# Eight of sixteen k-tile pairs of the down projection by the seven-product scheme instead of seven, in other places

## The chip, the core and the metric

The kernel runs on one core of a Trainium2 chip. Its engines are TensorE (PE: matrix products into PSUM; PEld is its loading of the stationary operand), VectorE (DVE), ScalarE (ACT), GpSimd (POOL) and SyncE (SP), which here only issues DMA transfers. The metric is the time of one execution on the device, in microseconds, and less is better.

## The reference

One decoder layer on 256 tokens with a width of 2048, all in float32. A recurrent branch and a sliding-window attention are merged and projected, and then comes the part that matters here, an MLP with a squared ReLU:

```python
h = rmsnorm(x, norm_mlp_pre[l])
u = jnp.square(jax.nn.relu(h @ w_mlp_up[l]))
x = x + rmsnorm(u @ w_mlp_down[l], norm_mlp_post[l])
```

`w_mlp_up` is 2048 x 8192 and `w_mlp_down` is 8192 x 2048. So the down projection sums over 8192 hidden channels, that is 64 k tiles of 128.

## The kernel before

**Products in three parts.** Every float32 operand is split into a rounded part (`hi`) and the remainder (`lo`), and a product is three matrix products: hi x hi, hi x lo and lo x hi (`product`, L1108). ScalarE rounds a weight half of 128 x 1024 (`whi`, L94), and VectorE subtracts to get the remainder (`wlo`, L95).

**The weight stream** (`Stream`, L54) handles the weights of the whole kernel in the order of their use. A weight chunk is 128 x 2048, which is two halves of 512 KB. SP loads a half into one of four raw buffers (`wraw`, L76), and the next load into that buffer can be issued only when the half has been split. The splits go to six `whi` and six `wlo` buffers, and `ahead` (L138) asks for the splits six halves ahead of the one in use. The four raw buffers mean that half j+4 is loaded into the buffer of half j.

**The MLP in two halves.** The hidden layer is done in two halves of 4096 channels (f = 0 and 1). Each half has an up projection of sixteen pairs of k tiles (`up_pair`, `a_pair`), whose results are squared and laid out by `evacuate` (L1090), and then two passes of the down projection (`down`, L1119), n = 0 and 1, for 1024 output columns each. So there are four passes. A pass goes through the sixteen pairs p = 0 to 15. The last two (14 and 15) are held back and multiplied at the end, one output quarter after the other, so that a quarter can be finished while the next is still being computed. The sums of the first half are written to DRAM (`acc_away`) and read back at the start of the first pass of the second half (L1215); the residual `x1` is read back near the end (L1226).

**Plain and seven-product pairs.** One pair p meets a 2 x 2 block problem: two token tiles by two k tiles times two k tiles by two column quarters. A plain pair takes 8 block products of three matmuls each, 24. A pair in `SEVEN` takes Strassen's scheme in Winograd's form: 7 block products, 21 matmuls. For this it needs sums of the weight blocks, and of the activation blocks:

```python
v.tensor_tensor(one..., b[:, l]..., a..., ALU.add)                 # L123, 1024 columns
v.tensor_tensor(b[:, l], t[:, l], a[:, r], ALU.add)                # L125, 512, in place
v.tensor_tensor(two, b[:, l], b[:, r], ALU.add)                    # L126, 512
self.nc.scalar.copy(hi, t)                                         # L129, 1536: thi
v.tensor_tensor(lo, t, hi.bitcast(F32), ALU.subtract)              # L130, 1536: tlo
```

These (`split_sums`, L114) stand beside the usual split of the two halves, of which the second is changed by L125. The sums `t` and their parts `thi` and `tlo` each take one of twelve large buffers (`unit`, L211, 8 KB a partition), which also hold the normalised input h2T (four), the plain pairs' activations (`rooms`, L1179), and in the last two passes the sums of the first half, the gain and `x1`. The three of `t` are used last in a pair: seven products in the order P1, Q3, P2, P6, Q4, Q5, N7 (L1112), and the last three take `thi` and `tlo`. The activations of a seven-product pair have seven blocks, with both parts, in tiles named `seven` (L1196), and `evacuate` makes their sums (L1101 to L1106).

Four products (P1, P6, Q5, N7) are kept in banks of their own through the pass. After the last pair of `SEVEN` they are combined (L1152 to L1156), in the second half the sums of the first are added (`early`, L1220), and each quarter is finished by one more addition (L1208, L1243, L1246).

**Order.** Each engine takes its instructions in a fixed order, made when the program is built by a scheduler from the order of the code and the buffers' release. `pin` keeps a few in the order of the code. An instruction that waits holds back all that stand behind it on its engine.

Of the kernel before, what the change touches and what calls it, by code (L numbers as in the profile page):

```python
# [19 lines left out]
F32R = mybir.dt.float32r  # L20
# [5 lines left out]
P = 128  # L26
# [9 lines left out]

WRAW, WHALF, T2, HELD = 4, 6, 8, 4

SEVEN = (0, 2, 4, 6, 8, 10, 12)
PAIRS = 16  # L40


# [124 lines left out]
def layer(tc, x, g_pre, pos_t, pos_row, inv_freq, vecs, sinks, gains, w_kv, w_q, w_xy, w_rg, w_g, w_rp, w_ap, w_out,  # L167
# [37 lines left out]
    for f in range(2):  # L205
        chunks += [w_up[32 * f + i] for i in range(32)]
        for n in range(2):
            sums.update(len(chunks) + i for i in SEVEN)
            chunks += [w_dn[(2 * f + n) * PAIRS + i] for i in range(PAIRS)]

    def unit(name, dt=F32R):  # L211
        return big.tile([P, 4, 2, S], dt, tag="U8", name=name)

    def flat(t):
        return t.rearrange("p a b c -> p (a b c)")
# [11 lines left out]
    def pump(n=1):  # L227

        for _ in range(n):
            while waiting:  # L230
                try:
                    next(waiting[0])
                    break
                except StopIteration:
                    waiting.pop(0)
# [7 lines left out]
    def a_pair(acts, out, prio=0):  # L243


        ps = pair("ps")

        def run(j, part, ks=range(8)):
            f, half = j // 2, j % 2
            for k in ks:  # L250
                kt = half * 8 + k
                a, w = acts[kt // 4][:, kt % 4], parts[j][part][:, k * P : k * P + P]
                if part:
                    mm(ps[:, f, 1, :], w, a[:, 0, :], start=False, stop=j == 1 and k == 7)  # L254
                else:
                    mm(ps[:, f].rearrange("p a b -> p (a b)"), w, a.rearrange("p a b -> p (a b)"), start=kt == 0,  # L256
                       stop=j == 3 and k == 7)

        at = ws.at
        parts = [ws.half()]
        run(0, 0)
        parts.append(ws.half(False))
        run(1, 0)
        pump()
        parts.append(ws.half(False))
        run(2, 0, (0,))
        run(0, 1)
        ws.ahead(at + 1)  # L270
        pump()
        run(1, 1)
        ws.ahead(at + 2)
        run(2, 1)
        parts.append(ws.half(False))
        run(3, 1)
        pump()
        run(2, 0, range(1, 8))
        ws.ahead(at + 3)
        run(3, 0)  # L280
        pump()
        with tc.high_priority(prio) if prio else ExitStack():
            nc.scalar.copy(out, ps[:, :, 1, :])
            nc.vector.tensor_tensor(out, ps[:, :, 0, :], out, ALU.add)
# [381 lines left out]
    def wide(t):  # L666
        return t.rearrange("p (f t) -> p f t", f=2)
# [208 lines left out]
    def u2(name):  # L876
        return pb.tile([P, 512], F32, tag="u2", bufs=4, name=name)
# [150 lines left out]
    for tb in range(TB):  # L1028
        for i in range(2):
            q = 2 + i  # L1030
# [3 lines left out]
    def up_pair(p, out):  # L1034

        ps = up_ps[p]
        for j in range(4 * p, 4 * p + 4):
            f, half = j // 2 % 2, j % 2
            kts = range(half * 8, half * 8 + 8)
            if j < 6:  # L1040
                lo = halves[j][1]
            else:
                hi, lo = ws.half()
                for kt in kts:
                    mm(ps[:, f].rearrange("p a b -> p (a b)"), hi[:, kt % 8 * P : kt % 8 * P + P],
                       h2T[kt // 4][:, kt % 4].rearrange("p a b -> p (a b)"), start=kt == 0, stop=False)
            for kt in kts:
                mm(ps[:, f, 1, :], lo[:, kt % 8 * P : kt % 8 * P + P], h2T[kt // 4][:, kt % 4, 0, :], start=False,
                   stop=kt == KT - 1)
            pump()  # L1050
        with tc.high_priority(PRIO):
            nc.scalar.copy(out, ps[:, :, 1, :])
            nc.vector.tensor_tensor(out, ps[:, :, 0, :], out, ALU.add)
# [28 lines left out]
    def spread_r2():  # L1082
        pr = bank(psb, "pr")
        for tb in range(TB):
            mm(pr[:, tb * P : tb * P + P], ones, diag[tb], start=True, stop=True)
        nc.scalar.copy(r2, pr[:, 0:S])
# [3 lines left out]
    def evacuate(p, u, dst):  # L1090
        nc.vector.scalar_tensor_tensor(wide(u), wide(u), 0.0, r2.unsqueeze(1).to_broadcast([P, 2, S]), ALU.max,
                                       ALU.mult)
        nc.scalar.activation(u, u, AF.Square)
        if p not in SEVEN:
            nc.scalar.copy(dst[:, :, 0, :], wide(u))
            nc.vector.tensor_tensor(dst[:, :, 1, :], wide(u), dst[:, :, 0, :].bitcast(F32), ALU.subtract)
            return

        e = u2("e")
        u4, e4 = [t.rearrange("p (a b) -> p a b", a=4) for t in (u, e)]  # L1100
        nc.vector.tensor_tensor(e4[:, 0:2], u[:, 0:P].unsqueeze(1).to_broadcast([P, 2, P]), u4[:, 1:3], ALU.subtract)  # L1101
        nc.vector.tensor_tensor(e4[:, 2], e4[:, 1], u4[:, 1], ALU.subtract)
        nc.vector.tensor_tensor(e4[:, 3], e4[:, 2], u4[:, 3], ALU.add)
        for to, of in ((dst[:, :, 0:3], u4[:, 1:4]), (dst[:, :, 3:7], e4)):
            nc.scalar.copy(to[:, 0], of)
            nc.vector.tensor_tensor(to[:, 1], of, to[:, 0].bitcast(F32), ALU.subtract)  # L1106

    def product(b, a, w, begun, tail=False):  # L1108

        for i, (x, y) in enumerate(((0, 0), (0, 1), (1, 0))):  # L1110
            mm(b, a[x], w[y], start=not begun and i == 0, stop=tail and i == 2)  # L1111
# [7 lines left out]
    def down(f, n, uT, held, order, finish, early, between=lambda p: None, behind=lambda: None):  # L1119
# [21 lines left out]
        for p in range(PAIRS - held):  # L1141
            if p in SEVEN:
                parts = ws.seven()
                for name, (i, w) in LEFT.items():
                    product(banks[name], (uT[p][:, 0, i], uT[p][:, 1, i]), parts[w], name in begun,
                            p == SEVEN[-1] and name in ("P1", "P6", "Q5", "N7"))
                    begun.add(name)
                if p == SEVEN[-1]:
                    for name in ((1, 0), (0, 0), (1, 1), (0, 1)):
# [27 lines left out]
    for f in range(2):  # L1177
        uT = {}
        rooms = [unit(f"uT{f}{i}") for i in range((PAIRS - len(SEVEN) + 1) // 2)]  # L1179
        full = []  # L1180
        for p in range(PAIRS):
            u = u2("u")
            if f == 0 and p < 2:
                up_pair(p, wide(u))
            else:
                a_pair(h2T, wide(u), PRIO if p == PAIRS - 1 else 0)
            full.append((p, u))
            if f == 0 and p == R2_AT:
                pump(99)
                spread_r2()  # L1190
                ctx3.close()
                pc = ctx2.enter_context(tc.tile_pool(name="pc", bufs=1))
            if f == 1 or p >= R2_AT:
                for q, u in full:
                    if q in SEVEN:
                        uT[q] = pc.tile([P, 2, 7, P], F32R, tag="seven", bufs=len(SEVEN), name=f"seven{f}{q}")  # L1196
                    else:
                        i = sum(k not in SEVEN for k in range(q))
                        uT[q] = rooms[i // 2][:, 2 * (i % 2) : 2 * (i % 2) + 2]
                    evacuate(q, u, uT[q])  # L1200
                full.clear()
# [142 lines left out]
```

## Time and profile before

| | us |
|---|---|
| three runs | 1510.14, 1512.02, 1512.23 (median 1512.02) |
| the profiled execution, whole | 1509.99 |
| its span, first to last instruction | 1508.2 |
| TensorE busy | 1492.7 |
| VectorE busy | 1101.7 |
| ScalarE busy | 828.7 |

The clock granted to TensorE was 0.998 of the full one. In the views, a row of the timeline gives the start, the duration, the engine, the line, the operation, the tiles written and read, and in brackets the idle time before it with what ended it. A row of the chain of work that ended last gives the start, the share of time on the chain, and what it was. A row of busy time by stretch gives the stretch, its length, and for PE, PEld, VectorE, ScalarE and GpSimd the busy time and the number of instructions, then the granted clock, the share of the DMA engines and GB/s. A matmul's listed duration is longer than the distance to the next one's start, since they overlap.

### The profile page before, as it was taken

What the parts mean: (1) busy time and instruction counts of PE and PEld (TensorE: products, weight loads), DVE (VectorE), ACT (ScalarE), POOL (GpSimd) and SP (SyncE); (2) the same over time, 40 slices, a digit from 0 to 9 for tenths busy, and PEclk for the clock granted to TensorE, in tenths of its full rate; (3) what the DMA queues carried; (4) which work ended last, traced back from release to release, by engine and by line L of the source; (5) the groups of instructions that cost most, each with busy time, mean ns of one, the idle gap of its engine ahead of it and who ended that gap; (6) DMA issues with size and microseconds to landing.
All of it is one profiled execution on the core that took longest, in us unless ns stands there. A gap on an engine that the chain in (4) does not pass through costs nothing.

```text
span 1508.2 us, 20012 instructions
## 1 busy us (share of the span) xinstructions
PE 1492.7 (99%) x7600; PEld 1261.5 (84%) x7600; DVE 1101.7 (73%) x1379; ACT 828.7 (55%) x1143; POOL 1.7 (0%) x9
## 2 busy tenths in 40 slices
PE   9999999999999999999999999999999999999997
PEld 7887787889888888888888888888888888888885
DVE  6675677858669966555667866698886666788897
ACT  6554665647566766443355655565454555555453
POOL 0000000000000000000000000000000000000000
PEclk9999999999999999999999999999999999999999
DMA  6645454465646566556764755566667565576665
GB/s 254 221 157 173 148 166 136 157 201 165 213 155 221 170 209 197 192 184 195 268 221 136 270 188 188 194 194 213 217 201 237 195 195 183 193 236 202 204 221 186
DMA packets 83327, 296.19 MB, mean 196 GB/s; under 512 B 9760, under 2 KB 10016, under 8 KB 82208
## 3 DMA queue, kind: packets, MB, share of 16 engines
q1 hardware_dynamic: 79920, 287.58, 57.6%
q10 hardware_dynamic: 3312, 7.35, 1.3%
q8 instruction: 59, 0.97, 0.3%
q14 instruction: 36, 0.29, 0.1%
HBM read 288.60 MB, written 6.29 MB: 196 GB/s over the span
## 4 chain that ended last, share of the span: by engine, by line
PE 84%; DVE 8%; DMA 4%; ACT 2%; issue 1%; DVEq 0%; SPq 0%; ACTq 0%
PE ps L256 21%; PE ps L254 11%; PE dQ L1111 5%; PE pp L298 4%; PE pp L294 4%; PE pp L296 4%; PE g L294 4%; DMA wraw<-in_w_dn 4%; PE g L298 4%; PE g L296 4%; DVE wlo L95 3%; PE s L1111 3%; PE dP L1111 2%; PE q L294 2%; PE q L298 2%; PE q L296 2%
## 5 line engine op out<-in xcount | busy, mean ns | idle before, releaser
L95 DVE TENSOR_TENSOR wlo<-wraw,whi 128x1024 fp32r<-128x1024 f32 x523 | 632.7, 1221 | 306.1 <-ACT whi L94 302.9
L94 ACT CAST whi<-wraw 128x1024 fp32r<-128x1024 f32 x523 | 544.2, 1052 | 554.0 <-PE ps L256 127.3
L256 PE MATMUL ps<-h2T,whi 128*128 128x512 f32 x960 | 223.9, 390 | 0.0
L256 PEld LDWEIGHTS ps<-h2T,whi 128*128 128x128 f32 x960 | 178.3, 188 | 35.6
L256 PE MATMUL ps<-hT,whi 128*128 128x512 f32 x512 | 121.3, 392 | 0.0
L254 PEld LDWEIGHTS ps<-h2T,wlo 128*128 128x128 f32 x960 | 119.1, 192 | 2.3
L254 PE MATMUL ps<-h2T,wlo 128*128 128x256 f32 x960 | 119.9, 283 | 0.0
L256 PEld LDWEIGHTS ps<-hT,whi 128*128 128x128 f32 x512 | 94.7, 188 | 19.8 <-issue 1.1
L1111 PE MATMUL dQ<-whi,uT 128*128 128x512 f32 x288 | 106.9, 389 | 0.0
L294 PE MATMUL g<-whi,hT 128*128 128x512 f32 x256 | 101.3, 396 | 0.0
L296 PE MATMUL g<-wlo,hT 128*128 128x512 f32 x256 | 100.1, 391 | 0.1
L298 PE MATMUL g<-whi,hT 128*128 128x512 f32 x256 | 99.9, 390 | 0.0
L254 PEld LDWEIGHTS ps<-hT,wlo 128*128 128x128 f32 x512 | 63.7, 192 | 1.8 <-issue 0.7
L254 PE MATMUL ps<-hT,wlo 128*128 128x256 f32 x512 | 64.7, 284 | 0.0
L1111 PEld LDWEIGHTS dQ<-whi,uT 128*128 128x128 f32 x288 | 54.1, 188 | 11.2
L294 PEld LDWEIGHTS g<-whi,hT 128*128 128x128 f32 x256 | 48.1, 188 | 10.5 <-issue 1.0
L296 PEld LDWEIGHTS g<-wlo,hT 128*128 128x128 f32 x256 | 48.1, 188 | 10.1 <-DVE wlo L95 0.5
L298 PEld LDWEIGHTS g<-whi,hT 128*128 128x128 f32 x256 | 48.1, 188 | 10.1
L1111 PE MATMUL dQ<-wlo,uT 128*128 128x512 f32 x144 | 56.1, 389 | 0.0
L1111 PE MATMUL dCs<-whi,uT 128*128 128x512 f32 x144 | 54.1, 389 | 0.0
L1111 PE MATMUL dP<-whi,uT 128*128 128x512 f32 x144 | 54.1, 389 | 0.0
L130 DVE TENSOR_TENSOR tlo<-t,thi 128x1536 fp32r<-128x1536 f32 x28 | 49.2, 1757 | 5.1 <-ACT thi L129 5.1
(285 smaller groups left out, 2461.6 us busy)
## 6 DMA issues: line engine op xcount, KB each, us to landing
wraw<-in_w_up SPq DMA_DIRECT2D x128, 512.0 KB, 3.9
wraw<-in_w_dn SPq DMA_DIRECT2D x128, 512.0 KB, 4.5
wraw<-in_w_g SPq DMA_DIRECT2D x64, 512.0 KB, 4.7
wraw<-in_w_xy SPq DMA_DIRECT2D x64, 512.0 KB, 3.7
wraw<-in_w_q SPq DMA_DIRECT2D x32, 512.0 KB, 4.3
wraw<-in_w_ap SPq DMA_DIRECT2D x32, 512.0 KB, 4.8
wraw<-in_w_rp SPq DMA_DIRECT2D x32, 512.0 KB, 4.6
wraw<-in_w_out SPq DMA_DIRECT2D x32, 512.0 KB, 4.9
```

Source lines behind the costliest of these rows:

```text
L94: self.pin(self.nc.scalar.copy(hi, src))
L95: self.pin(self.nc.vector.tensor_tensor(lo, src, hi.bitcast(F32), ALU.subtract))
L130: v.tensor_tensor(lo, t, hi.bitcast(F32), ALU.subtract)
L254: mm(ps[:, f, 1, :], w, a[:, 0, :], start=False, stop=j == 1 and k == 7)
L256: mm(ps[:, f].rearrange("p a b -> p (a b)"), w, a.rearrange("p a b -> p (a b)"), start=kt == 0, stop=j == 3 and k == 7)
L294: mm(banks[tb][n], a[:, 0, t], hi[:, n * 512 : n * 512 + 512], start=first, stop=False)
L296: mm(banks[tb][n], a[:, 0, t], lo[:, n * 512 : n * 512 + 512], start=False, stop=False)
L298: mm(banks[tb][n], a[:, 1, t], hi[:, n * 512 : n * 512 + 512], start=False, stop=last)
L1111: mm(b, a[x], w[y], start=not begun and i == 0, stop=tail and i == 2)
```

## The change

The tuple of seven-product pairs is replaced: 0, 2, 4, 6, 8, 10, 12 become 0, 1, 3, 5, 7, 9, 11, 13. In each of the four passes eight pairs take the scheme instead of seven; pairs 0 and 1 follow each other, and the last one is 13, directly ahead of the two held pairs. The places for the plain pairs' activations, two pairs to a unit, go from five units to four by the expression at L1179. The activation tiles of the first seven such pairs stay in their own buffers, and that of pair 13 takes a large unit, of which it uses seven of eight blocks. The layout of the weights in DRAM follows the tuple.

```diff
-SEVEN = (0, 2, 4, 6, 8, 10, 12)
+SEVEN = (0, 1, 3, 5, 7, 9, 11, 13)
+IN_POOL = 7
 PAIRS = 16
...
                     if q in SEVEN:
-                        uT[q] = pc.tile([P, 2, 7, P], F32R, tag="seven", bufs=len(SEVEN), name=f"seven{f}{q}")
+                        if SEVEN.index(q) < IN_POOL:
+                            uT[q] = pc.tile([P, 2, 7, P], F32R, tag="seven", bufs=IN_POOL, name=f"seven{f}{q}")
+                        else:
+                            uT[q] = flat(unit(f"seven{f}{q}")).rearrange("p (a b c) -> p a b c", a=2, b=8)[:, :, 0:7]
```

## The prediction

> **What bounds the kernel now.** I read the page first, then the busy time by stretch. The four down passes run from 980 to 1156 us and from 1333 to 1498 us.
>
> ```profile
> PE 1492.7 (99%) x7600; PEld 1261.5 (84%) x7600; DVE 1101.7 (73%) x1379; ACT 828.7 (55%) x1143; POOL 1.7 (0%) x9
> ...
> PE 84%; DVE 8%; DMA 4%; ACT 2%; issue 1%; DVEq 0%; SPq 0%; ACTq 0%
> ```
> ```profile
> 1156.00:1333.00 177.00, 177.00 (x1022) 156.84 (x1022) 124.00 (x147) 96.01 (x119) 0.00 (x0) 1.00 0.61 197
> 1333.00:1415.60 82.60, 82.60 (x365) 68.11 (x364) 70.22 (x69) 42.31 (x45) 0.00 (x0) 1.00 0.65 218
> 1415.60:1498.00 82.40, 82.40 (x365) 68.09 (x363) 72.97 (x77) 42.52 (x48) 0.00 (x0) 1.00 0.63 209
> 1498.00:1508.20 10.20, 0.20 (x1) 0.00 (x0) 5.86 (x11) 1.29 (x5) 0.00 (x0) 0.69 0.49 171
> ```
>
> TensorE never waits in a down pass, but VectorE is busy 85% to 89% of each of the last two. The chain that ended last, read in order of time, says more: it leaves TensorE at 1318.81 and does not come back.
>
> ```profile
> 1318.81 1.63 PE ps L256 x7
> ...
> 1412.37 3.85 DMA wraw<-in_w_dn
> ...
> 1423.91 5.19 DMA wraw<-in_w_dn
> ...
> 1429.23 1.23 DVE t L123
> 1430.45 1.14 DVE wlo L95
> 1431.59 0.61 DVE wraw L125
> ...
> 1432.36 1.06 ACT whi L94
> 1433.44 1.24 DVE wlo L95
> 1434.69 4.56 DMA wraw<-in_w_dn
> ...
> 1478.57 6.85 DMA wraw<-in_w_dn
> ...
> 1485.50 1.06 ACT whi L94
> ...
> 1499.51 0.61 DVE acc L1246
> ```
>
> This is a loop: a weight half lands, VectorE forms the sums of a seven-product pair, ScalarE rounds the second half, VectorE takes its remainder, and only that frees the raw buffer for the half four places on. One turn without the load is 5.44 us (1429.23 to 1434.67). In the tail VectorE, not TensorE, is last:
>
> ```profile
> 1497.81 0.39 PE L1111 MATMUL dQ<-whi,uT 128*128 128x512 f32 x1
> ```
> ```profile
> 1472.88 1.22 DVE L95 TENSOR_TENSOR wlo<-wraw,whi 128x1024 fp32r<-128x1024 f32 x1
> ...
> 1486.58 1.22 DVE L95 TENSOR_TENSOR wlo<-wraw,whi 128x1024 fp32r<-128x1024 f32 x1 [0.70 <-ACT whi L94]
> ...
> 1491.92 0.68 DVE L1246 TENSOR_TENSOR acc<-dQ,t 128x512 f32<-128x512 f32 x1
> ...
> 1499.42 0.68 DVE L1246 TENSOR_TENSOR acc<-dQ,t 128x512 f32<-128x512 f32 x1
> ```
>
> The last accumulation starts at 1499.42, 1.2 us after the last matmul ended (1497.81 + 0.39), because VectorE has been late since the last weight half. So a shorter TensorE stream alone brings nothing: VectorE must arrive earlier too.
>
> **The change, part by part.** (1) Matmuls. A seven-product pair has 21, a plain pair 24.
>
> ```profile
> 995.57 0.39 PE L1111 MATMUL dQ<-whi,uT 128*128 128x512 f32 x1
> ...
> 1001.01 0.39 PE L1111 MATMUL s<-whi,seven 128*128 128x512 f32 x1
> ...
> 1005.32 0.39 PE L1111 MATMUL s<-tlo,seven 128*128 128x512 f32 x1
> ```
> ```profile
> 1394.67 0.39 PE L1111 MATMUL s<-whi,seven 128*128 128x512 f32 x1
> ...
> 1399.43 0.39 PE L1111 MATMUL dQ<-whi,uT 128*128 128x512 f32 x1
> ...
> 1415.75 0.39 PE L1111 MATMUL s<-whi,seven 128*128 128x512 f32 x1
> ```
>
> A plain pair takes 5.44 us (995.57 to 1001.01), a seven-product pair 4.76 us (1394.67 to 1399.43), so 0.227 us a matmul. Four passes lose three matmuls each: 4 x 0.68 = 2.72 us of TensorE.
>
> (2) Work added. Back to back, VectorE starts its next instruction sooner than the listed duration:
>
> ```profile
> 1390.67 1.76 DVE L130 TENSOR_TENSOR tlo<-t,thi 128x1536 fp32r<-128x1536 f32 x1 [0.42 <-ACT thi L129]
> 1392.35 3.49 DVE L95 TENSOR_TENSOR wlo<-wraw,whi 128x1024 fp32r<-128x1024 f32 x3
> ...
> 1416.32 1.23 DVE L123 TENSOR_TENSOR t<-wraw,wraw 128x1024 f32<-128x1024 f32 x1 [0.85 <-DMA wraw<-in_w_dn]
> 1417.46 1.22 DVE L95 TENSOR_TENSOR wlo<-wraw,whi 128x1024 fp32r<-128x1024 f32 x1
> 1418.59 0.69 DVE L1243 TENSOR_TENSOR acc<-dCs,t 128x512 f32<-128x512 f32 x1
> 1419.19 1.22 DVE L95 TENSOR_TENSOR wlo<-wraw,whi 128x1024 fp32r<-128x1024 f32 x1
> ...
> 1422.67 2.35 DVE L95 TENSOR_TENSOR wlo<-wraw,whi 128x1024 fp32r<-128x1024 f32 x2
> 1424.94 1.75 DVE L130 TENSOR_TENSOR tlo<-t,thi 128x1536 fp32r<-128x1536 f32 x1
> 1426.61 1.22 DVE L95 TENSOR_TENSOR wlo<-wraw,whi 128x1024 fp32r<-128x1024 f32 x1
> ```
>
> From starts: 1.14 us for 1024 columns, 0.60 for 512, 1.67 for 1536. Each added pair gives VectorE one add of 1024, two of 512 and a remainder of 1536: 4.0 us a pass, 16 in all. No load, byte or SP issue is added; SP's order only follows the splits. ScalarE gains one rounding a pass, in gaps. The activations of the eighth pair add a few short VectorE operations per half of the hidden layer, inside the up projection (124 of 177 us busy there): nothing. Without that cover they would cost some 896 columns a half, about 1 us by the prices above and 1.5 with their starts (an estimate); the ends are 0 and 3 us for both halves. The eighth activation tile takes a large unit in place of the fifth of `rooms`; the count stays.
>
> (3) First half of the hidden layer. Three large units are free for `t`, `thi` and `tlo`, so pair 1's `thi` and `tlo` must take those of pair 0, and pair 1 follows at once. What such a handover costs is shown where the next pair reuses them today:
>
> ```profile
> 1005.75 1.49 ACT L129 CAST thi<-t 128x1536 fp32r<-128x1536 f32 x1 [0.41 <-PE s L1111]
> ```
>
> Pair 0's 20th matmul (the 1005.32 row there) releases `thi` 0.43 us after its start. Then 1.49 us of rounding and 1.76 us of remainder: 3.68 us after the 20th matmul's start, plus small gaps, pair 1's `tlo` is there. TensorE wants it at pair 1's 14th matmul, 15 places or 3.40 us after. So about 0.4 us is lost in each of the two passes; behind the waiting rounding, ScalarE's next roundings queue, and behind the remainder on VectorE the sums of pair 3; both are wanted only when pair 2's 5.44 us are over, and nobody waits. The bounds: 0.3 (no gap) to 1.8 (VectorE still in a remainder and an add before it). Net by the up projection's second half: 2 x (0.68 - 0.4) = 0.56 us saved, which shifts all that follows.
>
> (4) Second half, where the chain runs over VectorE. The first pass gives TensorE 0.68 us; five large units are free there, so no handover. Its last seven-product pair is now 13, not 12, and starts at 1399.43 instead of 1394.67, so its `tlo`, today done at 1392.43, ends 4.76 later, at 1397.2. Two remainders of pair 14 follow (1399.5) and free the buffer for the last half of the next pass's pair 0, which lands 4.6 us later (10.04 a turn, below, less 5.44): its sums start at 1404.1. From there to the end of pair 1's second remainder, VectorE's order holds six operations of 1024 columns, sixteen of 512 (two adds for each of two pairs, four that combine the products, four that add the earlier half, four that finish the quarters) and one of 1536: 6.84 + 9.60 + 1.67 = 18.1 us, to 1422.2. One remainder and pair 1's `tlo` end at 1425.1. TensorE starts this pass at 1415.07 and wants that `tlo` at 1415.07 + 4.76 + 13 x 0.227 = 1422.8: it waits 2.3 us, all in pair 1. Pair 0 was covered by 0.8 us.
>
> (5) The tail. Today the loop's second remainder ends at 1423.89 for pair 2 and at 1474.10 for pair 12: five turns, 10.04 us each. Now it ends at 1422.2 for pair 1 and needs six turns to pair 13: 1482.5. That frees the buffer of the last weight half, two pairs after. Today this buffer is free at 1478.57 and the half's remainder starts at 1486.58, 8.0 us later (the two loads of `x1` are issued right behind it); now it starts at 1490.5. Then come 1.14 us and eight operations of 0.60 (today seven, as one stood ahead) to the first accumulation: 1496.4 instead of 1491.92. VectorE is then busy without a gap that TensorE could fill, so the end moves by 4.5 us.
>
> Sum: 4.5 - 0.56 = 3.9 us on the profiled execution's 1509.99, or 1513.9. The three runs shown have the median 1512.02 and lie from 1510.14 to 1512.23, so executions come near 1510 and near 1512; I put the base between, at 1511.1, and forecast 1515.0.
>
> **The rivals.** A: TensorE is the bound, and its time goes with the matmuls. For it speaks the first row: 99% busy and no wait in a pass. Then 1511.1 - 2.7 = 1508.4, or 1507.2 if VectorE also loses its 1.2 us of lateness. Against it speaks the chain, off TensorE for the last 190 us. It decides if pair 1's sums are ready before TensorE wants them in all four passes. The Trainium skill's Perfetto Trace Analysis, Identifying the Most-Contended Engine, would have the most-contended engine optimized first; by occupancy that is TensorE, and this rule gives A. The order in time in this trace disagrees from 1318.81 on.
>
> B: the load in the loop is quicker when the splits run late. With the 3.85 us row a turn is 9.29, and six turns regain 4.5 us, all that the tail lost. TensorE then has -2.72 + 0.8 + 2.3 = +0.4, and the time is 1510.5 to 1511.5: no change. For it: that row; against: five turns of 10.04 in the same pass. The Trainium skill's DMA: Bandwidth & Descriptors, Anatomy of one DMA, fits 2.0 us plus bytes over 436 GB/s, for 512 KB an estimate of 3.2 us (for the GpSimd path); by it a turn is 8.6 us and the outcome is B. No load of the chain rows was that quick.
>
> C: the loop is slower still. With the 5.19 us row a turn is 10.63, and six cost 3.5 us more: 1518.5. The reload of the first half's sums (2 MB) falls into the first pass and could also hold a split.
>
> **How the numbers follow.** About 0.2% (3 us) is what a measurement of this kernel can tell from no change: 1508.1 and 1514.1. The forecast case has 0.52, with its own range 1513 to 1517, about three quarters of it above 1514.1; C has 0.16, B 0.19, A 0.13. Slower: 0.40 + 0.16 = 0.56. Faster: most of A, 0.11. Same: 0.33. The range goes from B's lower edge, rounded to 1509.5, to 1519.0 and leaves out most of A and a little of C. Predicted is the likeliest, 1515.0.
>
> **What would show it.** Right: 96 matmuls fewer on plain pairs and 84 more on seven-product pairs; `tlo` waits of TensorE of about 0.4 us at the second pair of both passes of the first half and about 2 us in the last pass; the first accumulation of the tail near 1496; the chain still on loads and VectorE. Wrong: TensorE without a wait in the last pass, or turns of under 9.5 us, or the last accumulation starting at most 1 us after the last matmul.

## The result, and the profile after

The changed kernel takes 1522.47 us (median of four runs, 1520.26 to 1526.29) against 1512.01 for the kernel before: a ratio of 1.0078, 95% interval 1.0057 to 1.0098. Slower, as predicted, but by 10.5 us where 3.9 were predicted, and outside the predicted range. The profiled execution is the longest of the four, 1526.29 us with a span of 1524.2; so what a trace shows as lost adds up to more than the 10.5 us between the medians. Its lines L95, L96, L124 to L131 and L1112 are L94, L95, L123 to L130 and L1111 of before, and L1212 and L1213 are the finishing addition of the first half (L1208) and the write of its result to `acc_away`. In the other runs the lines move by a few more; the tiles name the operation.

The page of the changed kernel, busy time and shares of the chain that ended last:

```profile
PE 1495.7 (98%) x7588; PEld 1260.2 (83%) x7588; DVE 1120.2 (73%) x1403; ACT 833.5 (55%) x1149; POOL 1.7 (0%) x9
...
PE 80%; DVE 10%; DMA 5%; ACT 3%; issue 2%; DVEq 0%; ACTq 0%; SPq 0%
```

TensorE has its twelve matmuls less and is nevertheless busy 3.0 us longer: some of its matmuls ran slowly. Its waits, by what ended them (total, times, longest), name operations that never held it before:

```profile
PE dQ L1112 <- DVE tlo L131: 3.2, 4, 1.6
PE dQ L1112 <- ACT thi L130: 2.7, 1, 2.7
PE dQ L1112 <- DVE wlo L96: 2.4, 1, 2.4
...
PE s L1112 <- DVE wlo L96: 1.7, 2, 1.1
```

Busy time by stretch says where (columns as before):

```profile
1060.00:1070.00 10.00, 7.62 (x34) 6.00 (x33) 6.06 (x8) 4.26 (x5) 0.00 (x0) 1.00 0.48 170
1080.00:1090.00 10.00, 6.70 (x23) 4.72 (x22) 8.32 (x8) 4.27 (x4) 0.00 (x0) 0.81 0.66 236
1090.00:1100.00 10.00, 10.00 (x39) 8.04 (x38) 9.30 (x10) 5.63 (x6) 0.00 (x0) 0.85 0.59 205
...
1415.60:1498.00 82.40, 77.94 (x336) 62.26 (x335) 76.33 (x78) 43.73 (x46) 0.00 (x0) 1.00 0.60 199
1498.00:1524.20 26.20, 14.03 (x62) 11.27 (x61) 19.20 (x31) 5.02 (x12) 0.00 (x0) 0.85 0.42 159
```

There are three holes: 2.4 us at the end of the first pass, 3.3 us at the start of the second with a lowered clock behind it, and about 4.5 us in the last. Two of the three lie in the first half of the hidden layer, where the prediction had expected a small gain. The timeline of the changed kernel shows both:

```profile
1064.14 1.23 DVE L124 TENSOR_TENSOR t<-wraw,wraw 128x1024 f32<-128x1024 f32 x1 [3.91 <-DMA wraw<-in_w_dn]
...
1066.02 1.22 DVE L96 TENSOR_TENSOR wlo<-wraw,whi 128x1024 fp32r<-128x1024 f32 x1
...
1067.29 0.50 PE L1112 MATMUL dQ<-wlo,uT 128*128 128x512 f32 x1 [2.38 <-DVE wlo L96]
...
1075.93 0.92 ACTq L1213 DMA_DIRECT2D acc_away<-t  x2
1076.97 1.06 ACT L95 CAST whi<-wraw 128x1024 fp32r<-128x1024 f32 x1 [7.56 <-DVE t L1212]
...
1083.95 1.04 ACT L95 CAST whi<-wraw 128x1024 fp32r<-128x1024 f32 x1 [2.09 <-DMA wraw<-in_w_dn]
1084.90 1.47 ACT L130 CAST thi<-t 128x1536 fp32r<-128x1536 f32 x1
...
1086.40 1.76 DVE L131 TENSOR_TENSOR tlo<-t,thi 128x1536 fp32r<-128x1536 f32 x1
1086.42 0.80 PE L1112 MATMUL dQ<-thi,seven 128*128 128x512 f32 x1 [2.73 <-ACT thi L130]
...
1088.21 0.80 PE L1112 MATMUL dQ<-tlo,seven 128*128 128x512 f32 x1 [0.57 <-DVE tlo L131]
```

At the end of the first pass the remainder of the last held half (1066.02) stands on VectorE behind the sums of the next pass's pair 0, which wait 3.91 us for their load; TensorE wants that remainder at about 1064.7. At the start of the second pass `thi` of pair 1 could start at about 1080.8, when pair 0's 20th matmul has released its buffer (the pass starts at 1076.04, 19 matmuls follow, and the release takes the 0.43 us of the prediction), but on ScalarE it stands behind the rounding of a half four places on (1083.95), which waits for a load. That load waited for a raw buffer, that buffer for a remainder, and that for the rounding at 1076.97, which stood behind two issues of `acc_away`; e7 below takes these away. The chain of work that ended last has the two slowest loads there and in the tail:

```profile
1057.46 6.56 DMA wraw<-in_w_dn
...
1494.41 6.17 DMA wraw<-in_w_dn
```

In both places of the first half something that is ready stands in an engine's fixed order behind a half that is not yet loaded.

**How the runs are read below.** The table is worked out from the starts of all matmuls of the four passes in each profiled execution: the length of a pass less 0.2267 us for each of its matmuls (82.28 / 363 in the kernel before). That is what the pass lost to waits and to slow matmuls. The last column runs from the start of the last matmul to the end. The saving of work, 0.68 us for each pass with eight pairs, comes on top. A row describes one execution, and the executions of one kernel differ by up to 7 us (e7: 1521.19 to 1528.57), so the rows say where a kernel loses, and the medians how much.

| run | median us | ratio to before, 95% interval | lost, passes 1 / 2 / 3 / 4 | to the end |
|---|---|---|---|---|
| before | 1512.01 | | 0 / 0 / 0.3 / 0 | 10.4 |
| changed | 1522.47 | 1.0078 (1.0057 to 1.0098) | 2.9 / 6.6 / 0 / 6.6 | 12.6 |
| e8 new places, first half only | 1516.69 | 1.0040 (1.0025 to 1.0055) | 1.5 / 7.3 / 0.2 / 0 | 10.9 |
| e13 second half only | 1520.52 | 1.0069 (1.0055 to 1.0083) | 0 / 0 / 1.0 / 8.9 | 12.7 |
| e1 0,2,..,12,13 | 1522.57 | 1.0074 (1.0059 to 1.0089) | 0.3 / 0 / 2.1 / 9.1 | 12.7 |
| e2 0,1,3,..,11 | 1514.56 | 1.0022 (1.0012 to 1.0031) | 0 / 2.5 / 0 / 1.4 | 10.0 |
| e10 1,3,..,13 | 1513.15 | 1.0015 (1.0007 to 1.0024) | 0 / 0 / 0 / 0.9 | 10.9 |
| e3 couples | 1532.84 | 1.0142 (1.0127 to 1.0157) | 5.7 / 4.2 / 2.0 / 10.4 | 12.8 |
| e4 short turn | 1539.18 | 1.0186 (1.0167 to 1.0204) | 8.3 / 2.4 / 9.6 / 7.3 | 12.7 |
| e7 acc on GpSimd | 1523.80 | 1.0091 (1.0068 to 1.0113) | 0.3 / 6.0 / 0 / 5.0 | 12.9 |
| e9 thi first | 1520.54 | 1.0065 (1.0049 to 1.0080) | 1.4 / 2.0 / 0 / 9.8 | 12.6 |
| e14 thi first, first half only | 1513.39 | 1.0020 (1.0011 to 1.0029) | 1.0 / 2.0 / 0.6 / 0 | 9.9 |
| e5 changed, fifth buffer | 1509.74 | 0.9992 (0.9982 to 1.0001) | 0.3 / 0.3 / 0 / 1.0 | 10.0 |
| e6 before, fifth buffer | 1511.09 | 1.0002 (0.9993 to 1.0011) | 0 / 0 / 0.8 / 0 | 9.9 |
| e11 as e1, fifth buffer | 1508.40 | 0.9983 (0.9974 to 0.9991) | 0.4 / 0 / 0.7 / 0 | 10.0 |
| e12 0,2,..,8,9,11,13, fifth buffer | 1510.68 | 1.0002 (0.9994 to 1.0011) | 0.3 / 0 / 2.1 / 0.8 | 11.8 |
| e15 as e1, first half only | 1511.34 | 1.0003 (0.9994 to 1.0012) | 0.3 / 1.8 / 0.2 / 1.1 | 11.8 |

The kernel before was measured anew with each group of runs (1510.4 to 1512.0); each ratio is to its own.

### The profile page after: what moved, and what is told of

It reads as the page before. It is cut to its first block, busy times and chain, and to the rows that moved or that the text cites. A ratio compares the mean times of both kernels' runs of the same rounds, so it can differ in the third digit from the quotient of the medians.

```text
span 1524.2 us, 20022 instructions
## 1 busy us (share of the span) xinstructions
PE 1495.7 (98%) x7588; PEld 1260.2 (83%) x7588; DVE 1120.2 (73%) x1403; ACT 833.5 (55%) x1149; POOL 1.7 (0%) x9
## 4 chain that ended last, share of the span: by engine, by line
PE 80%; DVE 10%; DMA 5%; ACT 3%; issue 2%; DVEq 0%; ACTq 0%; SPq 0%
PE ps L257 22%; PE ps L255 11%; DMA wraw<-in_w_dn 5%; DVE wlo L96 4%; PE pp L297 4%; PE pp L295 4%; PE pp L299 4%; PE g L295 4%; PE g L297 4%; PE g L299 4%; PE dQ L1112 3%; PE q L295 2%; PE q L299 2%; PE q L297 2%; PE s L1112 2%
## 5 line engine op out<-in xcount | busy, mean ns | idle before, releaser
L96 DVE TENSOR_TENSOR wlo<-wraw,whi 128x1024 fp32r<-128x1024 f32 x523 | 631.9, 1220 | 295.0 <-ACT whi L95 293.1
L95 ACT CAST whi<-wraw 128x1024 fp32r<-128x1024 f32 x523 | 543.3, 1052 | 554.5 <-PE ps L257 115.9
L1112 PE MATMUL dQ<-whi,uT 128*128 128x512 f32 x256 | 95.2, 391 | 0.0
L131 DVE TENSOR_TENSOR tlo<-t,thi 128x1536 fp32r<-128x1536 f32 x32 | 56.2, 1756 | 6.2 <-ACT thi L130 6.0
L1112 PEld LDWEIGHTS dQ<-whi,uT 128*128 128x128 f32 x256 | 48.3, 189 | 10.1
L299 PEld LDWEIGHTS g<-whi,hT 128*128 128x128 f32 x256 | 48.1, 188 | 10.1
L1112 PE MATMUL dQ<-wlo,uT 128*128 128x512 f32 x128 | 50.2, 392 | 2.4 <-DVE wlo L96 2.4
L124 DVE TENSOR_TENSOR t<-wraw,wraw 128x1024 f32<-128x1024 f32 x32 | 39.1, 1222 | 17.5 <-DMA wraw<-in_w_dn 17.3
L295 PE MATMUL q<-whi,hT 128*128 128x512 f32 x128 | 51.0, 399 | 0.0
```

Of the source, the lines that this page charges most:

```text
L95: self.pin(self.nc.scalar.copy(hi, src))
L96: self.pin(self.nc.vector.tensor_tensor(lo, src, hi.bitcast(F32), ALU.subtract))
L124: v.tensor_tensor(one.rearrange("p (a b) -> p a b", a=2), b[:, l].unsqueeze(1).to_broadcast([P, 2, 512]), a.rearrange("p (a b) -> p a b", ...
L295: mm(banks[tb][n], a[:, 0, t], hi[:, n * 512 : n * 512 + 512], start=first, stop=False)
L299: mm(banks[tb][n], a[:, 1, t], hi[:, n * 512 : n * 512 + 512], start=False, stop=last)
```

## The experiments

Three theories stood at the start. **Ring:** the loads wait for one of four raw buffers, and what stands behind a half not yet loaded waits with it. **Work:** the eighth pair's VectorE operations are too many. **Handover:** an adjacent pair waits for its neighbour's `thi` and `tlo`. The first expectations call the first two the loop and the count theory.

### Places and number of the pairs (e1, e2, e3, e10)

```diff
-SEVEN = (0, 1, 3, 5, 7, 9, 11, 13)
+SEVEN = (0, 2, 4, 6, 8, 10, 12, 13)    # e1
+SEVEN = (0, 1, 3, 5, 7, 9, 11)         # e2
+SEVEN = (0, 1, 4, 5, 8, 9, 12, 13)     # e3
+SEVEN = (1, 3, 5, 7, 9, 11, 13)        # e10
```

e1: 

> Eight pairs as in the changed kernel, at 0, 2, 4, 6, 8, 10, 12, 13: the first two no longer adjacent, the last two adjacent instead. Before is 1512.0, changed 1522.5. Count theory (the 4 us of VectorE work that an eighth pair adds to each pass): the same work, so again about 1520 to 1525. Loop theory (one turn from load to load of about 10 us for each seven-product pair, and two turns must fit between pair 13 of one pass and pair 1 of the next): here the turns between passes are as far apart as before, 13 only adds its own work, so 2.7 us less TensorE work and at most some 4 us lost in the tail: 1508 to 1514. Handover theory (thi and tlo of an adjacent pair wait for its neighbour): one adjacent pair in each pass stays, only elsewhere, so 1518 or more.

Measured: 1522.57, the time that the work theory gave, and within what the handover theory allowed (1518 or more). The passes say more: without the couple 0, 1 the first half loses 0.3 us instead of 9.6, with the same eight pairs; the last pass loses 9.1. So in the first half the number is not the cause; in the second the run does not tell number from ring. My expectation for the ring theory (1508 to 1514) was over 8 us too low.

e2: 

> Seven pairs at 0, 1, 3, 5, 7, 9, 11: the adjacent start of the changed kernel without its eighth pair. TensorE's work is that of the kernel before. Count theory: seven pairs, so about 1512. Handover theory: the adjacent pairs 0 and 1 cost as in the changed kernel, 1518 to 1524. Loop theory: from pair 11 of a pass to pair 1 of the next there are 4.76 + 4 x 5.44 + 4.76 = 31.3 us of TensorE for two turns, as in the kernel before (12 to 2: 31.3), so 1510 to 1514, and the tail ends earlier than before since four plain pairs stand behind the last.

Measured: 1514.56, just above what the ring theory gave and far under the handover theory's 1518. Seven pairs that start with a couple lose 2.5 us, all at pair 1 of the second pass, and 1.4 in the last pass. The couple costs something, but without the eighth pair the kernel is 2.9 us slower than its own before, about a quarter of the whole.

e3: 

> Eight pairs at 0, 1, 4, 5, 8, 9, 12, 13: all in adjacent couples with two plain pairs between. Handover theory: four adjacent couples in a pass instead of one, so the loss of the changed kernel (10 us) grows to about four times in the first half's passes: 1530 or more. Count theory: eight pairs, 1520 to 1525. Loop theory: the second half of a seven-product pair follows in the ring of raw buffers on that of a plain pair, whose turn is short (load about 4.5, one rounding, one remainder), so a pass makes up lateness by some 3 us in each couple; the place between the passes (13, then 0 and 1) stays as tight as in the changed kernel: 1513 to 1519.

Measured: 1532.84, as the handover theory had it and against my ring expectation. Each of the four couples waits in the first pass, at its 15th matmul for `tlo`, 1.12 to 1.23 us from start to start beyond the usual distance. So a handover costs up to 1.2 us, three times the 0.4 of the prediction; couples make up no lateness. In the changed kernel's first pass the one couple cost 0.24 in all.

e10: 

> Seven pairs at 1, 3, 5, 7, 9, 11, 13: the last one is 13 as in the changed kernel, but none are adjacent and there are no more than before. Ring theory: from pair 13 of a pass to pair 1 of the next there are 4.76 + 3 x 5.44 = 21.1 us of TensorE, as in the kernel before from 12 to 0, so no pass has waits of more than 1 us in all; the tail is later since only two plain pairs stand behind 13: 1511 to 1515. Last-place theory (the four combining additions and the four that add the first half's sums now fall among the held pairs' remainders and the next pass's sums, and that alone makes the last pass late): waits in the last pass of 3 us or more and the tail 2 us longer: 1516 to 1520.

Measured: 1513.15, as the ring theory had it. A last place of 13 alone does not make the last pass late (0.9 us).

### Which half (e8, e13)

```diff
-SEVEN = (0, 1, 3, 5, 7, 9, 11, 13)
+SEVENS = ((0, 1, 3, 5, 7, 9, 11, 13), (0, 2, 4, 6, 8, 10, 12))    # by f; e8, the other way round in e13
```

e8: 

> The new places (0, 1, 3, 5, 7, 9, 11, 13) in the first half's two passes only; the second half has the seven pairs of the kernel before. By the trace of the changed kernel its first half loses 9.6 us to waits and slow matmuls and saves 1.4 of work, so if that loss is made there, 1512 + 8 = 1520 (1516 to 1522), and the second half adds only the rest. If instead the cause is VectorE's work in the last passes and the tail, as predicted, this kernel is at 1510 to 1513.

e13: 

> The new places in the second half's two passes only; the first half has the seven pairs of the kernel before. Before is 1511, changed 1522.5, first half alone 1516.7 (+5.7). If the losses add up, this one is at +5: 1515 to 1517.5. If the second half's chain of raw buffers takes its own time from its start on, and part of its lateness was hidden by TensorE's lateness from the first half, this one alone loses more: 1518 to 1521. As predicted (4.5 us in the tail, less 1.4 of saved work that the waits eat up): 1514 to 1517.

Measured: the first half alone costs 1516.69 - 1510.80 = 5.9 us, the second alone 1520.52 - 1510.44 = 10.1, both together 10.5. They do not add up; the second of e13's three ranges, 1518 to 1521, had allowed for that. In the changed kernel the last pass begins 7.5 us later than in e13 (1423.70 against 1416.16) but the sums of its pair 0 begin only 5.2 us later (1415.07 against 1409.90), so TensorE's earlier lateness hides part of VectorE's.

Of e13 the chain of work that ended last (start, time on the chain):

```profile
1333.54 7.33 DMA wraw<-in_w_dn
...
1346.54 7.28 DMA wraw<-in_w_dn
...
1384.44 1.22 DVE t L124
...
1389.91 4.26 DMA wraw<-in_w_dn
...
1394.29 1.23 DVE t L124
...
1403.94 5.86 DMA wraw<-in_w_dn
```

The chain of the kernel before has the sums of its last seven-product pair, 12, at:

```profile
1385.43 1.24 DVE t L123
```

The timeline of e13:

```profile
1399.89 1.76 DVE L131 TENSOR_TENSOR tlo<-t,thi 128x1536 fp32r<-128x1536 f32 x1 [0.15 <-ACT thi L130]
...
1409.90 1.23 DVE L124 TENSOR_TENSOR t<-wraw,wraw 128x1024 f32<-128x1024 f32 x1 [3.20 <-DMA wraw<-in_w_dn]
...
1418.23 2.36 DVE L96 TENSOR_TENSOR wlo<-wraw,whi 128x1024 fp32r<-128x1024 f32 x2
...
1419.51 0.65 PE L1114 MATMUL s<-wlo,seven 128*128 128x512 f32 x1 [2.97 <-DVE wlo L96]
1419.96 0.63 PE L1114 MATMUL s<-whi,seven 128*128 128x512 f32 x1
...
1422.77 1.23 DVE L124 TENSOR_TENSOR t<-wraw,wraw 128x1024 f32<-128x1024 f32 x1
...
1502.85 0.68 DVE L1253 TENSOR_TENSOR acc<-dQ,t 128x512 f32<-128x512 f32 x1
```

Two loads at the start of the half take 7.3 us: the reload of the first half's sums (2 MB, issued at 1333.8 and 1337.8) falls there. That does not set the two kernels apart: the kernel before has the same reload (issued at 1339.1 and 1339.5), with a load of 8.20 us on its chain beside it (1346.48). What does, on the chain, is the number of turns. The sums of pair 11 (1384.44) are here no later than those of pair 12 before (1385.43); both are the seventh in their pass. The eighth, of pair 13, come a whole turn later, at 1394.29: the load (1389.91) waited for pair 11's last remainder. The load that ends in the sums of the next pass's pair 0 takes 5.86. Then the first remainder of pair 0 (1418.23) stands on VectorE behind its pair's three additions, the four combining ones, the four that add the first half's sums and two of the finishing ones, and TensorE waits at its second matmul. This wait was not in the prediction, which followed the list only to pair 1.

### Orders on ScalarE and VectorE (e4, e7, e9, e14)

e4 puts the remainders of a seven-product pair behind its three additions:

```diff
-        v.tensor_tensor(two, b[:, l], b[:, r], ALU.add)
-        ahi, alo = self.two_parts(a, j)
-        bhi, blo = self.two_parts(b, j + 1)
+        behind = v.tensor_tensor(two, b[:, l], b[:, r], ALU.add).ins
+        with self.tc.issue_after(behind):
+            ahi, alo = self.two_parts(a, j)
+            bhi, blo = self.two_parts(b, j + 1)
```

> The changed kernel with one order changed on VectorE: in a seven-product pair the remainders of its two halves come behind the three additions, so the second half is changed and rounded about 1.1 us sooner and its remainder ends some 0.6 us sooner; the work is the same. Loop theory: each turn is about 0.6 us shorter, a pass makes up 4 to 5 us, the waits at the end of the first pass (2.4 us) and of the last pass's later pairs go, those at the start of a pass shrink: 1510 to 1516. Count and handover theories: the same work in the same places, 1520 to 1525.

Measured: 1539.18, 17 us worse, which no theory had. Its chain and its stretches:

```profile
1020.00 1.24 DVE t L124
...
1024.98 6.00 DMA wraw<-in_w_dn
1031.11 1.24 DVE t L124
```
```profile
1022.60 4.62 DVE L96 TENSOR_TENSOR wlo<-wraw,whi 128x1024 fp32r<-128x1024 f32 x4
```
```profile
1024.90:1031.00 6.10, 6.10 (x29) 5.05 (x28) 3.99 (x4) 2.60 (x3) 0.00 (x0) 1.00 0.82 297
```

From the sums to the second remainder a turn did get shorter, 4.98 us (1020.00 to 1024.98) against 5.44 in the prediction's loop. But now four remainders follow each other and free four raw buffers within 5 us, and the loads into them on its chain take 5.4 to 6.1 us, with the DMA engines busy at 0.82 in the stretch shown; those on the changed kernel's chain over the same turns take 4.7 to 5.5. Over four turns of the first pass (1009.48 to 1052.90) a turn takes 10.86 us; in the changed kernel (1008.09 to 1049.72) 10.41. The loads are not a constant. That bunching them is what makes each slower fits these rows; no run varies it alone. That the work is the same and the time 17 us longer speaks against the work theory.

e7 issues the writes of the sums from GpSimd:

```diff
-                    nc.scalar.dma_start(acc_away[tb][:, c], t)
+                    nc.gpsimd.dma_start(acc_away[tb][:, c], t)
```

> The changed kernel with the four writes of the first half's sums issued from GpSimd's queue instead of ScalarE's, so no rounding on ScalarE stands behind an issue that waits for VectorE's finishing add. Ring theory: the rounding of pair 1's first half, today held until 1076.97, starts about 2 us earlier, so the load behind it and the rounding of pair 1's sums that stands behind that half come 2 us earlier; of the 4.6 us of waits at pair 1 of the second pass 2.5 stay, and the 2 us lost to slow matmuls behind them go: 1517 to 1520. VectorE work and handover theories: 1520 to 1525, as VectorE's work and the buffers are the same.

Measured: 1523.80, no gain; a miss for the ring theory (1517 to 1520). The rounding came earlier, its remainder hardly:

```profile
1071.34 1.06 ACT L95 CAST whi<-wraw 128x1024 fp32r<-128x1024 f32 x1 [5.38 <-PE dCs L1112]
...
1074.90 1.21 DVE L96 TENSOR_TENSOR wlo<-wraw,whi 128x1024 fp32r<-128x1024 f32 x1
...
1081.10 1.04 ACT L95 CAST whi<-wraw 128x1024 fp32r<-128x1024 f32 x1 [4.32 <-DMA wraw<-in_w_dn]
1082.05 1.47 ACT L130 CAST thi<-t 128x1536 fp32r<-128x1536 f32 x1
```

The rounding ends at 1072.4, but the remainder that frees the raw buffer starts at 1074.90, behind finishing adds on VectorE. Counted from the pass's first matmul (1073.14 here, 1076.04 in the changed kernel) it is only 0.5 us earlier, and a wait of 2.79 us at pair 1 stays (2.73 in the changed kernel).

e9 lets `thi` of an adjacent pair go ahead of the half four places on:

```diff
+        p = j // 2 - 2
+        with self.tc.issue_after(self.thi[p]) if p in self.thi and p - 1 in self.sums else ExitStack():
-        self.pin(self.nc.scalar.copy(hi, src))
+            self.pin(self.nc.scalar.copy(hi, src))
...
-        self.nc.scalar.copy(hi, t)
+        self.thi[j // 2] = self.nc.scalar.copy(hi, t).ins
```

> The changed kernel (1522.5) with one place in ScalarE's order changed: the rounding of an adjacent pair's sums (thi of pair 1) stands ahead of the rounding of the half four places on, which waits for its load, instead of behind it. In the changed kernel's second pass thi of pair 1 could start at 1080.6, when pair 0's 20th matmul has released its buffer, but starts at 1084.90 behind that half. Queue theory: the wait of 4.6 us at pair 1 of the second pass falls to under 1 us, the 2 us of slow matmuls behind it go, the last pass stays: 1515 to 1518. Handover theory (the buffer itself is what pair 1 waits for): nothing changes, 1520 to 1525. VectorE work theory: nothing changes either, as VectorE has the same operations.

Measured: 1520.54, above the queue theory's 1515 to 1518. The timeline of e9:

```profile
1079.87 1.48 ACT L133 CAST thi<-t 128x1536 fp32r<-128x1536 f32 x1
1081.98 1.04 ACT L98 CAST whi<-wraw 128x1024 fp32r<-128x1024 f32 x1 [0.64 <-DMA wraw<-in_w_dn]
...
1416.79 0.39 PE L1116 MATMUL s<-whi,seven 128*128 128x512 f32 x1
1420.38 0.79 PE L1116 MATMUL s<-wlo,seven 128*128 128x512 f32 x1 [3.21 <-DVE wlo L99]
```

The second pass loses 2.0 instead of 6.6 us, so its wait was that order and not the buffer. But the last pass loses 9.8 instead of 6.6, with a new wait of 3.2 us at pair 0, the one of e13. The time is no clear gain. e14 is the same reordering in e8, with nothing behind it to give the gain back:

> The new places in the first half only, and thi of pair 1 ahead of the half four places on in ScalarE's order. Without the reordering it was 1516.7, of which the trace shows 7.3 us lost in the second pass. Queue theory with the gain given back by the second half: here nothing gives it back, so 4 to 5 us less: 1511 to 1513.5. If the reordering only moves the wait to another place in the same pass: 1515 to 1518.

Measured: 1513.39, as expected, against 1516.69 in e8, about 3 us less (ratios 1.0020 and 1.0040). The gain in the second pass is real, and in e9 the second half took most of it.

### A fifth raw buffer (e5, e6, e11, e12), and e15

```diff
-                t = self.pool.tile([P, 1024], F32, tag="wraw", bufs=WRAW, name=f"wraw{j}")
+                if self.fifth and j % 5 == 0:
+                    t = self.fifth.tile([P, 1024], F32, tag="wraw5", bufs=1, name=f"wraw{j}")
+                else:
+                    t = self.pool.tile([P, 1024], F32, tag="wraw", bufs=WRAW, name=f"wraw{j}")
...
-        self.load_to(max(2 * EXTRA, j + WHALF) + WRAW)
+        self.load_to(max(2 * EXTRA, j + WHALF) + WRAW + (self.fifth is not None))
...
+                ws.fifth = pc
...
```

e5: 

> The changed kernel with a fifth raw buffer from the down projections on (4 KB a partition, found by moving the two diagonal tiles and the tile of ones), so the load of half j waits for the split of half j-5 instead of j-4; all work stays. Changed is 1522.5. Ring theory (lateness comes from the loads that wait for a raw buffer, and everything that stands behind a half not yet loaded waits with it): the second half of a seven-product pair now follows on a first half, whose remainder is done some 3 us earlier, so the turn of about 10 us has 3 us of slack; of the 9.6 us that TensorE loses in the first half's passes at most 2 stay, of the 6.6 us in the last pass at most 3: 1506 to 1513. VectorE work theory: the same operations on VectorE, so the last pass stays as late and the time falls by less than 3 us: 1519 to 1524. Handover theory (thi and tlo of pair 1 wait for those of pair 0): the wait at pair 1 of the second pass stays at some 5 us: 1516 to 1520.

Measured: 1509.74, 12.7 us less than the changed kernel (11.5 when each is compared with its own before), with the same operations on VectorE in the passes (busy 1119.5 us, 1120.2 in the changed kernel). The one wait of TensorE that the view lists in the passes, and ScalarE at the start of the second pass:

```profile
PE dQ L1118 <- DVE tlo L135: 0.5, 1, 0.5
```
```profile
1075.40 2.01 ACT L99 CAST whi<-wraw 128x1024 fp32r<-128x1024 f32 x2 [0.43 <-PE dQ L1118]
1078.54 1.48 ACT L134 CAST thi<-t 128x1536 fp32r<-128x1536 f32 x1 [1.14 <-PE s L1118]
```

`thi` of pair 1 now waits for TensorE's release and for nothing else, as the prediction had assumed, and the couple costs 0.25 us in each pass of the first half. The ring theory stands as the cause; work and handover, which gave 1519 to 1524 and 1516 to 1520, are excluded as the main one. Its prices do not stand as well: in e1, e2, e3, e4 and e7 the time that I expected by it was too low, by 0.6 to 23 us. The Trainium skill's Perfetto Trace Analysis, Optimization Strategy, says that the same gap, repeating on the engine that should be saturated, can mean that there is no room for the next tile. The gaps here differ in place and length, but the traces agree with the remedy: the passes lost 2.9 + 6.6 + 6.6 = 16.1 us with four buffers and 0.3 + 0.3 + 1.0 = 1.6 with five.

e6, the control: 

> The kernel before with the same fifth raw buffer, as the control of the run above. No pass of it has a wait of TensorE, so all theories expect little: at most the lateness of VectorE in the tail goes, 1508 to 1512.

Measured: 1511.09, no change. The buffer is worth nothing where no wait was.

e11, `SEVEN` of e1 with the fifth buffer: 

> Eight pairs at 0, 2, 4, 6, 8, 10, 12, 13 with the fifth raw buffer. Without it these places cost 1522.6, with waits of 7.9 us in the last pass. Ring theory: those waits go as in the changed kernel with the fifth buffer (6.6 to 1.0): 1507.5 to 1511. VectorE work theory: the last pass, with 13 directly behind 12, still waits: 1514 or more.

Measured: 1508.40, faster than both kernels: 0.9983 (0.9974 to 0.9991). That is 2.7 us under its own before (1511.11), as much as TensorE's whole saving of work. Its busy time by stretch and the shares of its chain:

```profile
1333.00:1414.00 81.00, 80.59 (x356) 66.42 (x355) 72.38 (x72) 43.51 (x46) 0.00 (x0) 1.00 0.67 224
1414.00:1496.00 82.00, 82.00 (x364) 67.84 (x362) 78.25 (x84) 43.15 (x49) 0.00 (x0) 1.00 0.62 205
```
```profile
PE 94%; DVE 3%; ACT 1%; issue 1%; DMA 0%; SPq 0%; DVEq 0%; ACTq 0%
```

VectorE is busy 95% of the last pass (78.25 of 82.00) and holds TensorE nowhere in it; the chain is TensorE's again.

e12, `SEVEN = (0, 2, 4, 6, 8, 9, 11, 13)` with the fifth buffer: 

> Eight pairs at 0, 2, 4, 6, 8, 9, 11, 13 with the fifth raw buffer: the adjacent couple lies in the middle of the pass, where the splits have had four pairs to run ahead, instead of at its start. With the couple at the start 1.0 us was still lost in the last pass and 0.25 us at the couple in each of the first half's passes. Ring theory: the 1.0 us goes, the 0.25 us stay, TensorE saves its 2.7 us: 1507 to 1509.5, faster than both kernels. VectorE work theory: as the run with the couple at the start, 1509 to 1511.

Measured: 1510.68, a miss for the ring theory and within what the work theory gave (1509 to 1511), though that theory had failed at e11, where it gave 1514 or more. The last pass's wait went (0.8 us stayed, at `tlo` of pairs 4 and 9), but the third pass lost 2.1 us, 1.25 of it at the held pairs, and the tail was 1.8 us longer than in e11. Why is open.

e15, `SEVENS` with e1's places in the first half and before's in the second, four buffers: 

> Eight pairs at 0, 2, 4, 6, 8, 10, 12, 13 in the first half only, seven as before in the second, four raw buffers. In the run with these places in all passes the first half lost 0.25 us and saved 1.36 us of work. If a saving in the first half reaches the end: 1509 to 1510.5. If the chain of loads in the second half does not follow TensorE's earlier start: 1510.5 to 1512.

Measured: 1511.34, no difference from before. In this execution the second pass lost 1.8 us, which in e1 it had not, so the run does not show whether a saving in the first half would reach the end.

## Why the prediction was right or wrong

**The sign and the chain.** The time rose, and because of the loop it named: a load that waits for a raw buffer, sums, rounding, remainder; the fifth raw buffer takes the loss away (e5) and does nothing where no wait was (e6). The sign rests on the second half alone: for the first the prediction had a saving, which was wrong. The turn was right: six turns from pair 1 to pair 13 of e13's last pass take 10.18 us each (1422.77 to 1483.85), 10.04 were predicted. TensorE's own two pairs take 4.76 + 5.44 = 10.20 us, though, so that pass does not tell which of the two sets the pace. Rival A fails: TensorE's shorter stream would have given 1508.4. B fails: the loads on the chain of the changed kernel's last pass took from 4.27 to 6.17 us, none the 3.85 that it needed. C was nearest in time, at 1518.5, and too small; its slower turn of 10.63 us did not come. None of the three signs of being wrong appeared, as all three look for a smaller loss: the last accumulation starts 3.4 us after the last matmul's end (1515.46 against 1512.03), not within 1 us.

**Steps (1) and (2)** hold in their counts: 7588 matmuls; VectorE is busy 18.5 us more, against 16 predicted and 2 to 3 for the activations of both halves. That ScalarE's added rounding falls "in gaps" does not hold at the start of the second pass. (The first matmul of the down passes is at 990.81, not 980, as the prediction read; nothing hangs on it.)

**Step (3) failed**, the first half. It priced the handover a little too high where it stood alone: 0.24 us lost in the first pass, 0.4 predicted with 0.3 and 1.8 as bounds (e3's couples cost up to 1.2). But it said that what queues behind the waiting rounding is wanted late and nobody waits, and put the loop of loads at nothing in this half. Here too the eighth pair took a turn more: the sums of pair 13 start 58.2 us after the first matmul of the pass, 9.4 later than those of pair 12 before, where TensorE reaches its pair only 4.8 later. The prediction did not ask what stands ahead of the waiting rounding: at the start of the second pass, a half whose load is late, shown by e9 and e14. Nor did it ask what stands behind the next pass's sums at the end of the first: the last held half's remainder. That wait goes with how late these sums start, counted from the first matmul of the pass: 72.6 us and 2.4 us of wait in the changed kernel, 71.2 to 71.8 and at most 1 in e8, e9 and e14, 69.4 and none in e7. In e1 the remainder stands ahead of the sums, which start at 72.2, and nothing waits. Instead of 0.56 us saved, the first half alone cost 5.9.

**Step (4) failed in the time of pair 13's split.** The prediction let pair 13's `tlo` end 4.76 us after that of pair 12 today, because TensorE starts pair 13 by so much later. But the split goes by its own loop, one turn for each seven-product pair, as step (5) counts it: pair 13 is the eighth, and its sums start at 1394.29 in e13, 9.85 us after pair 11's and 8.9 after those of pair 12 before. So its `tlo` ended at 1401.65 (1399.89 + 1.76) instead of 1397.2, 4.5 us later, and the load behind it took 5.86 instead of 4.6. The sums of the last pass's pair 0 were predicted to start at 1404.1, earlier than the 1407.00 of the kernel before, and start at 1409.90, 5.8 later. From there on the step's list of VectorE's work was right: pair 1's `tlo` ended at 1430.87, again 5.8 after the predicted 1425.1. "Pair 0 was covered by 0.8 us" fell with the late start: TensorE waits 3.0 there, and matmuls at half speed follow.

**Step (5)**, the tail, inherited this: the first accumulation was predicted at 1496.4 and came at 1502.85. Of those 6.5 us, 5.8 are the late start and six turns of 0.14 the rest. The step itself, six turns from a late start, was right. The 4.5 us forecast for the second half and the 5.8 of step (4) make 10.3, and 10.1 were measured.

**The sum** added the halves. Measured they are 5.9 (where -0.56 was predicted) and 10.1 (4.5), and together 10.5. So the miss of 6.6 us in the time is two larger misses, of 6.5 and 5.6, less what the one half hides of the other.

## What to carry to other kernels

When a chain runs through a ring of buffers, price it by its turn, its start and the number of turns, never by the starts of the engine that it feeds, and at each wait ask what stands ahead of the waiting instruction on its engine as well as behind it: a ready operation behind one that waits for a load cost more here than the buffer conflict that was priced. Try one more buffer before reordering: 4 KB a partition took away over 11 us, while of the three reorderings two gave nothing or worse, as each moved a bunch of loads or a wait elsewhere. A loss found in an early stage need not come back when it is mended, if a later stage was hidden by it.

## What the runs showed of the hardware that was not expected

**After a wait of about 3 us the matmuls run at half rate, for 3.41 or 6.83 us.** In the changed kernel the matmuls from 1086.42 on follow each other at 0.43 us instead of 0.227, and the granted clock is 0.81 and 0.85 in the two stretches shown; taken from 1086.22 to 1093.05 it is 0.50. Such a stretch came with waits of TensorE of 2.73 us (changed), 2.79 (e7 and e8), 2.97 (e13), 3.21 (e9), 3.31 and 5.21 (e4). Its length does not follow that of the wait: it was 6.83 us with the waits of 2.73, 3.21 and 3.31 and with e8's, and 3.41 with those of 2.97 and 5.21 and with e7's. In the changed kernel, e13 and e9 it cost 2.0 to 3.1 us beyond the wait, with 10 to 13 lengthened distances. After the wait of 2.38 us in the first pass none came (only one matmul was longer there, 0.50 instead of 0.39). The length of the wait alone does not decide: in the 3.41 us directly before each of these drops TensorE was busy at most 1.2 us; counted back from 1086.22 in steps of 3.41 us, the wait of 2.38 us falls into two such steps, in which TensorE was busy 2.58 and 1.86 us. The Trainium skill's TensorE: Matmul & The Clock Gate, Part 1: The HAM clock gate, has the clock halve after at least one idle window of about 3.4 us; the traces agree on the half rate, but in them some 2.2 us of idle time out of 3.41 were enough (e7 and e9).

**A load of 512 KB on the chain took from 4.3 to 7.3 us in one run.** In e13:

```profile
1333.50:1341.00 7.50, 7.50 (x34) 6.20 (x34) 4.14 (x6) 4.72 (x7) 0.00 (x0) 1.00 0.81 298
1389.90:1394.00 4.10, 4.10 (x20) 3.40 (x19) 3.97 (x3) 2.96 (x4) 0.00 (x0) 1.00 0.55 180
1403.90:1410.00 6.10, 6.10 (x28) 5.07 (x27) 2.48 (x4) 2.59 (x3) 0.00 (x0) 1.00 0.89 250
```

With the DMA engines busy at 0.55 the load of the chain took 4.26 us, at 0.81 and 0.89 it took 7.33 and 5.86. The share alone does not give the time: in the kernel before a load took 3.58 us at 0.69 (1337.8 to 1341.4) and one 8.20 at 0.76 (1346.5 to 1354.7). The prediction used one duration for all. The Trainium skill's DMA: Bandwidth & Descriptors, Anatomy of one DMA, by which a load alone would take some 3.2 us (an estimate, for the GpSimd path), has no term for what else is under way. The quickest load read on a chain here took 3.58 us, and the measured loads decide.
